# A two-layer attention backbone: the last head of three attention stages put in another order

## The chip, the cores and the metric

The kernel runs on one core of one Trainium2 chip. The time is the device time of one execution in microseconds. A profile of one further execution shows what each engine did; the engines are PE (matrix products), DVE and POOL (elementwise work), ACT (activations and copies) and SP (it issues most DMAs).

## The reference, cut to what matters

512 latent tokens and 256 context tokens of width 1024 go through two layers. In each layer one projection feeds two attentions: A, a two-dimensional neighbourhood attention with 8 heads, and B, a grouped-query attention with 8 query heads and 2 key-value heads. Latent queries also read the context's keys. Both results are multiplied by a SiLU gate, projected, merged and projected again. The context tokens run through layer 0 alone.

```python
def _merge(a_att, b_att, a_z, b_z, g_a, g_b, w_o_a, w_o_b, w_out):
    o_a = (a_att * jax.nn.silu(a_z)) @ w_o_a
    o_b = (b_att * jax.nn.silu(b_z)) @ w_o_b
    merged = jax.nn.sigmoid(g_a) * o_a + jax.nn.sigmoid(g_b) * o_b
    return merged @ w_out

def _layer(x, ctx, ...):
    ...
    a_att = _na_latent(qa, ka, va, cka, cva, rpb, rows)
    ...
    b_att = _gqa_latent(qb, k_all, v_all)
    out_x = _merge(a_att, b_att, a_z, b_z, g_a, g_b, w_o_a, w_o_b, w_out)
    x_new = x + gate_x * out_x
    if update_ctx:
        ...
        ctx = ctx + gate_c * out_c
    return x_new, ctx
```

All is float32. The kernel splits each operand of a product into a high part in a narrower format, and a low part (operand minus high part), and sums three products: high by high, high by low, low by high.

## The kernel before, in words

**Tiles.** A tile of activations has 128 partitions, on which channels or tokens lie. The nine `big` tiles (128 x 3072 floats) hold whole tensors and are handed out again when their last reader is done. Weights come in pieces of 128 x 512: a DMA into `raw` (three buffers), a cast on ACT into the high part `whi`, a subtraction on DVE or POOL into the low part `wlo` (eight buffers each, tags in the pool `wp`). PSUM has eight banks: one for `psf`, two for transposes (`pst`), and five that each stage shares out anew. In the neighbourhood stage that is one `psx`, three for scores (`pss`) and one for values (`psv`); in the grouped stage two score tiles of two banks and one `psv`; in projections five `psx`.

**Layer.** Projections of keys, values and queries come first, then the neighbourhood stage, the projections for the grouped stage, the grouped stage, then the merge: four chunks of the projection of B (`o_chunks("b", ...)`), each of two groups of output channels, and the output projection. Gate projections and the projection of A are `fill`: pieces that stand between the heads so that PE has work.

**A stage's heads.** `pipeline` runs the scores of head h, then the values of head h-1, then some fill. Scores go to a bank; DVE takes the maximum, ACT the exponential, and the normalisation (`softmax_tail`) is on POOL for two of the four query tiles and on DVE for the others. The values of a head need the probabilities transposed: PE writes four transposes into a bank, ACT casts them (`pth`), DVE subtracts (`ptl`): `transpose_split`, 3 to 6 times a head, with two buffers of each tag. Then come the products with the value tensor into `psv`, and `head_out`: ACT copies one half of the bank (`ho`), DVE adds the other half, and the sum is multiplied into the gated tensor (`za` for A, `zb` for B; line 699). The one `psv` bank is free for the next head after the add. In layer 0 each head also has the values of the context queries (`ctx_values`), in the same bank.

**The end of a stage.** After the last head's scores the grouped stage calls `early`: it loads the gate tensors `tg[1]` and `tg[3]`, takes the tiles `gbh` and `gbl` (high and low part of the gated B), and splits the first three quarters of `zb` into them (`hilo`, lines 559 to 569), high parts on ACT, low parts on POOL. Then come the last head's values, and the last quarter. In layer 1's grouped end, and only there, every second split of the last head goes to a score bank and to weight tiles (`spare`), and the product of `head_out` is on DVE. There the chunk weights after the first are also held behind the last head-out's copy on ACT.

**Order.** A planner puts the instructions of each engine in one fixed order, from the program's order and its own costs. `ordered(i, last)` makes it place an instruction behind another one of the same engine. Tiles that don't fit yet wait for the last reader of an older one.

Of the kernel before, what the change touches and what calls it, by code (L numbers as in the profile page):

```python
# [12 lines left out]
ALU = mybir.AluOpType  # L13
# [55 lines left out]
def hybrid_kernel(es: ExitStack, tc, x, ctx, cvec, w_ada, w_ada0, small, gvec, w_in, w_o_a, w_o_b, w_out,  # L69
# [421 lines left out]
    def layer(l, hx, nxt, mid):  # L491
# [67 lines left out]
        def hilo(src, dst, fs, parts=None, lo=lambda f: G, hi_after=None, lo_after=None):  # L559
            sv = src.rearrange("p (f n) -> p f n", f=4)  # L560
            ins = nc.cur_bb.bb.instructions
            for f in fs:
                for a, b in parts or [(0, ntok)]:
                    S.copy(R(dst[0][:, f, a:b]), sv[:, f, a:b])
                    if hi_after is not None and f > 0:
                        ordered(ins[-1], hi_after)
                    lo(f).tensor_tensor(R(dst[1][:, f, a:b]), sv[:, f, a:b], dst[0][:, f, a:b], ALU.subtract)
                    if lo_after is not None and lo(f) is G:
                        ordered(ins[-1], lo_after)
# [4 lines left out]
        def o_chunks(br, prepare, evac):  # L574

            src = (w_o_a if br == "a" else w_o_b)[l]
            act = lambda part, k: gated[br][part][:, k, :]
            res = []
            for i in range(4):
                st = {}  # L580

                def ld(i=i, st=st):
                    st["w"] = load_w2(src, 256 * i, 4, mix_lo)
                pieces = [lambda f=f, n0=n0, n1=n1, i=i, st=st:
                          chan_proj(st["w"], f, act, n0, n1, lambda f, a, b, ps: evac(2 * i + f, a, b, ps))
                          for f in range(2) for n0, n1 in spans]
                res.append((ld, ([prepare] if i == 0 and prepare else []) + pieces))
            return res

# [71 lines left out]
        if True:  # L661
# [11 lines left out]

            def transpose_split(blocks, n0=0, n1=512):

                spare = att["end"] and not first and att["turn"] % 2 == 1
                att["turn"] += 1
                pt = psw(512, "s" if spare else "t")
                for src, c0 in blocks:
                    if c0 is None:  # L680
                        T.transpose(pt.rearrange("p (s n) -> p s n", n=64)[:, 0:8:7, :], src, ident)
                    else:
                        T.transpose(pt[:, c0:c0 + 128], src, ident)  # L683
                pool, th, tl, n = (wp, "whi", "wlo", 8) if spare else (att["p"], "pth", "ptl", att["nt"])
                hi = pool.tile([128, 512], F32R, tag=th, name=nm(th), bufs=n)
                lo = pool.tile([128, 512], F32R, tag=tl, name=nm(tl), bufs=n)
                S.copy(hi[:, n0:n1], pt[:, n0:n1])  # L687
                V.tensor_tensor(lo[:, n0:n1], pt[:, n0:n1], F(hi[:, n0:n1]), ALU.subtract)  # L688
                return hi, lo

            def head_out(po, e, dst):

                n = dst.shape[-1]
                m, o = 64 * e, 64 * (1 - e)
                t1 = att["p"].tile([128, 512], F32, tag="ho", name=nm("ho"), bufs=1)
                S.copy(t1[m:m + 64, :n], po[o:o + 64, :n])
                att["ho"] = nc.cur_bb.bb.instructions[-1].name
                V.tensor_tensor(t1[m:m + 64, :n], po[m:m + 64, :n], t1[m:m + 64, :n], ALU.add)
                (V if (att["end"] and not first) else G).tensor_tensor(dst, dst, t1[m:m + 64, :n], ALU.mult)

            def rows(a, half):
                return a[64 * half:64 * half + 64]
# [53 lines left out]
            def ctx_values(p, vsl, dst, e):  # L756
                hi, lo = transpose_split(
                    [(p[:, 256 * i + 128 * k:256 * i + 128 * k + 128], 256 * k + 128 * i)
                     for k in range(2) for i in range(2)])
                po = psw(256, "v")  # L760
                for k in range(2):
                    T.matmul(po, vsl(4 + k), hi[:, 256 * k:256 * k + 256], start=k == 0, stop=False)
                    T.matmul(po, vsl(4 + k), lo[:, 256 * k:256 * k + 256], start=False, stop=k == 1)  # L763
                head_out(po, e, dst)
# [34 lines left out]
            def na_scores(h, q, kh, kl):  # L799
                load_bias(h)  # L800
                ps_ = []
                for i in range(4):
                    pss = ps_score()
                    qi = q[:, 128 * i:128 * i + 128]
                    at = ((0, 3, 2), (0, 1, 2), (1, 2, 1), (4, 1, -2))[i]
                    for k, b in ((kh, True), (kl, False)):
                        T.matmul(pss.rearrange("p (a b n) -> p a b n", a=2, b=2), qi, blocks_of(k, *at), start=b, stop=not b)  # L807
                    p = p_tile()
                    mx = sp.tile([128, 2], F32, tag="mx", name=nm("mx"), bufs=8)
                    four = lambda a: a.rearrange("p (a b n) -> p a b n", a=2, b=2)  # L810
                    V.tensor_tensor_reduce(four(p[:, :512]), four(pss),
                                           blocks_of(bedg if i == 0 else bint, 0, 1, 1) if i in (0, 2) else four(bint),
                                           -1.0, 3e38, ALU.add, ALU.min, mx[:, 0:1])
                    r = sp.tile([128, 2], F32, tag="r", name=nm("r"), bufs=8)
                    S.activation(p[:, :512], p[:, :512], AF.Exp, bias=mx[:, 0:1], scale=-1.0,
                                 accum_out=r[:, 0:1])
                    softmax_tail(p, 512, r[:, 0:1], [(0, 512)], G if i in NA_POOL else None)
                    ps_.append(p)
                    run(att["bg"], 1)
                return ps_  # L820
# [32 lines left out]
            def pipeline(fill, spread, scores_of, values_of, last=None, bg=[]):  # L853
# [2 lines left out]
                prev = None  # L856
                for h in range(8):
                    att["bg"] = bg if h > 3 or pm["n"] == 1 else []
                    st = scores_of(h)
                    if prev is not None:  # L860
                        values_of(h - 1, prev)
                    run(fill, len(fill) - (n - n * min(h + 1, spread) // spread))
                    prev = st
# [1 line left out]
                    run(fill, len(fill))  # L865
                    last()
                run(bg, len(bg))
                att["end"] = last is not None
                values_of(7, prev)
                run(fill, len(fill))  # L870

            akt = [k_tile(e, True) for e in range(2)]
            att["end"], att["turn"] = False, 0

            def na_first(h):
                j, e = h // 2, h % 2
# [3 lines left out]
                ps_ = na_scores(h, q, kh, kl)  # L880
                return ps_, ctx_scores(q, kh, kl, 256) if first else None

            def values_of(dst, f):
                def g(h, st):
                    vsl = f(h, st[0])
                    if first:
                        e = h % 2
                        zv = dst.rearrange("p (f n) -> p f n", f=4)
                        ctx_values(st[1], vsl, zv[64 * e:64 * e + 64, h // 2, 512:768], e)
                return g  # L890
# [74 lines left out]
            def gq_scores(q, kh, kl):  # L965
                ps_ = []
                for i in range(4):
# [5 lines left out]
                    V.tensor_reduce(mx[:, 0:1], pss, AX, ALU.max, negate=True)  # L973
                    r = sp.tile([128, 2], F32, tag="r", name=nm("r"), bufs=8)
                    S.activation(p, pss, AF.Exp, bias=mx[:, 0:1], accum_out=r[:, 0:1])
                    softmax_tail(p, 768, r[:, 0:1], [(0, 768)], G if i in GQ_POOL else None)
                    ps_.append(p)
                    run(att["bg"], 1)
                return ps_

            def gq_values(h, ps_):
                e, kv = h % 2, h // 4

                def vsl(t):
                    return R(vb[:, t, kv, 64 * e:64 * e + 128])
# [15 lines left out]

            def early():

                for c in (1, 3):
                    tg[c] = big("tg")
                    load_tg(c)
                gated["b"] = hilo_tiles("gb")
                hilo(zb, gated["b"], range(3), lo_after=None if first else att["norm"])
            bg = gate_steps((1,), att["p"]) if first else []
            pipeline(fill, 8, gq_first, values_of(zb, gq_values), early, bg)  # L1010
            gq_es.close()

        with tc.tile_pool(name=f"mrg{l}", bufs=1, reuse_waits="tile") as mp:
# [254 lines left out]
```

## Time and profile before

| | |
|---|---|
| median of 3 runs | 1142.38 us (1141.61 to 1142.96) |
| the profiled execution | 1141.48 us |
| its span, from the first to the last instruction | 1139.6 us |
| busy share of the span | PE 98%, DVE 72%, ACT 51%, POOL 43% |
| granted clock of PE | 0.999 |

A row of a timeline or of the chain of waits begins with its start and its length in microseconds. A name such as `gbl<-zb,gbh` gives the tile written and the tiles read; `xcount` means that neighbours of one kind are merged. A bracket at the end tells how long the engine sat idle before the row, and what ended that. A row of the waits has the waiting engine and tile, what it waited for, the total, the count and the longest.

### The profile page before, as it was taken

The numbers are of one execution on the slowest core, as the hardware profiler recorded it, in microseconds if no ns is written. First come the engines' busy times: TensorE is split into PE (matmuls) and PEld (weight loads), VectorE is DVE, ScalarE is ACT, GpSimd is POOL, SyncE is SP. The second block draws the span as 40 slices with busy tenths as digits, with TensorE's granted clock in tenths as the row PEclk, the third lists the DMA queues.
The fourth block names the chain that finished last, engine by engine and source line by source line (L and its number), as shares of the span: only waits on it lengthen the run. The fifth ranks groups of instructions, "written<-read, shape, count | busy, mean of one in ns | idle before, by whom it ended". The sixth has DMA issues, their size and how long they took to land.

```text
span 1139.6 us, 17434 instructions
## 1 busy us (share of the span) xinstructions
PE 1119.0 (98%) x6128; PEld 947.5 (83%) x6128; DVE 816.4 (72%) x1537; ACT 581.1 (51%) x1185; POOL 492.7 (43%) x467
## 2 busy tenths in 40 slices
PE   7999999999999999999999999999999999999998
PEld 5788888888988888888888887888887988888777
DVE  6777688887554786698588755569787666798783
ACT  6553366665433565666330365337666445665531
POOL 2073354544374343353512427246553664363521
PEclk9999999999999999999999999999999999999999
DMA  9645222333333232461343524634332333141343
GB/s 370 238 127 157 81 61 70 97 115 98 114 102 89 91 108 87 80 242 38 137 141 102 176 75 116 188 91 125 103 111 74 112 94 110 66 157 38 99 163 99
DMA packets 90863, 135.09 MB, mean 119 GB/s; under 512 B 10804, under 2 KB 55064, under 8 KB 90136
## 3 DMA queue, kind: packets, MB, share of 16 engines
q1 hardware_dynamic: 88640, 127.57, 35.2%
q0 software_dynamic: 1856, 6.29, 1.7%
q8 instruction: 48, 0.79, 0.3%
q14 instruction: 39, 0.32, 0.1%
q10 hardware_dynamic: 280, 0.12, 0.0%
HBM read 116.63 MB, written 17.32 MB: 118 GB/s over the span
## 4 chain that ended last, share of the span: by engine, by line
PE 86%; DVE 5%; DMA 3%; issue 3%; POOL 2%; ACT 1%; SPq 0%; POOLq 0%; ACTq 0%; DVEq 0%
PE psx L352 12%; PE psx L354 12%; PE psx L353 12%; PE psf L352 10%; PE psf L354 10%; PE psf L353 10%; PE pst L683 5%; PE pss L807 3%; PE pss L734 2%; PE pss L735 2%; PE psv L990 2%; PE psv L991 2%; PE pst L432 1%; DMA rawb<-in_w_ada_dram 1%; DVE ptl L688 1%
## 5 line engine op out<-in xcount | busy, mean ns | idle before, releaser
L687 ACT CAST pth<-pst 128x512 fp32r<-128x512 f32 (+1 forms) x173 | 97.2, 576 | 96.4 <-PE pst L683 56.0
L688 DVE TENSOR_TENSOR ptl<-pst,pth 128x512 fp32r<-128x512 f32 (+1 forms) x173 | 113.8, 671 | 41.1 <-ACT pth L687 40.0
L339 POOL TENSOR_TENSOR wlo<-raw,whi 128x512 fp32r<-128x512 f32 x68 | 95.9, 1414 | 104.4 <-ACT whi L337 86.2
L352 PE MATMUL psf<-hx,whi 128*128 128x512 f32 (+1 forms) x368 | 140.1, 381 | 0.0
L353 PE MATMUL psf<-hx,whi 128*128 128x512 f32 (+1 forms) x368 | 138.0, 375 | 0.0
L352 PE MATMUL psx<-whi,hx 128*128 128x512 f32 (+1 forms) x368 | 137.8, 375 | 0.0
L354 PE MATMUL psf<-hx,wlo 128*128 128x512 f32 (+1 forms) x368 | 137.7, 374 | 0.0
L354 PE MATMUL psx<-whi,hx 128*128 128x512 f32 (+1 forms) x368 | 135.9, 369 | 0.0
L353 PE MATMUL psx<-wlo,hx 128*128 128x512 f32 (+1 forms) x368 | 135.3, 368 | 0.0
L337 ACT CAST whi<-raw 128x512 fp32r<-128x512 f32 x136 | 82.5, 621 | 55.9 <-DMA raw<-in_w_in_dram 36.5
L322 ACT CAST whi<-raw 128x512 fp32r<-128x512 f32 x88 | 54.0, 622 | 100.9 <-PE psx L354 35.3
L683 PE MATMUL pst<-ident,p 128*128 128x128 f32 x628 | 97.7, 272 | 0.8 <-DVE r L664 0.6
L669 POOL TENSOR_SCALAR r<-r 128x1 f32<-128x1 f32 x64 | 22.3, 348 | 164.1 <-DVE r L664 139.4
L339 DVE TENSOR_TENSOR wlo<-raw,whi 128x512 fp32r<-128x512 f32 x68 | 67.1, 989 | 32.9 <-ACT whi L337 32.6
L325 POOL TENSOR_TENSOR wlo<-raw,whi 128x512 fp32r<-128x512 f32 x36 | 50.7, 1413 | 85.6 <-ACT whi L322 72.4
L683 PEld LDWEIGHTS pst<-ident,p 128*128 128x128 f32 x628 | 76.4, 140 | 12.3 <-PE psv L763 0.7
L670 POOL TENSOR_TENSOR p<-p,r 128x512 f32<-128x512 f32 (+1 forms) x64 | 84.3, 1317 | 5.1
L352 PEld LDWEIGHTS psx<-whi,hx 128*128 128x128 f32 x368 | 69.4, 189 | 12.2 <-issue 1.2
L354 PEld LDWEIGHTS psx<-whi,hx 128*128 128x128 f32 x368 | 69.4, 189 | 12.0 <-DVE hx L1165 0.2
L354 PEld LDWEIGHTS psf<-hx,wlo 128*128 128x128 f32 x368 | 69.3, 188 | 11.8
L353 PEld LDWEIGHTS psx<-wlo,hx 128*128 128x128 f32 x368 | 69.5, 189 | 10.7
L352 PEld LDWEIGHTS psf<-hx,whi 128*128 128x128 f32 x368 | 69.4, 189 | 10.4 <-ACT zt L517 0.2
(265 smaller groups left out, 3068.6 us busy)
## 6 DMA issues: line engine op xcount, KB each, us to landing
raw<-in_w_in_dram SPq DMA_DIRECT2D x168, 256.0 KB, 2.9
rawb<-in_w_ada_dram SPq DMA_DIRECT2D x48, 256.0 KB, 2.9
gs<-zt SPq DMA_DIRECT2D x32, 256.0 KB, 2.0
raw<-in_w_out_dram SPq DMA_DIRECT2D x32, 256.0 KB, 3.0
tg<-gs SPq DMA_DIRECT2D x4, 1536.0 KB, 6.5
rawx<-in_w_ada_dram SPq DMA_DIRECT2D x8, 512.0 KB, 7.7
raw<-in_w_o_a_dram SPq DMA_DIRECT2D x16, 256.0 KB, 2.9
raw<-in_w_o_b_dram SPq DMA_DIRECT2D x16, 256.0 KB, 4.3
```

What stands on the lines that cost most here:

```text
L322: S.copy(hi[:, :n], raw[:, :n])
L325: e.tensor_tensor(lo[:, :n], raw[:, :n], F(hi[:, :n]), ALU.subtract)
L337: S.copy(hi, raw)
L339: lo_eng(i).tensor_tensor(lo, raw, F(hi), ALU.subtract)
L352: T.matmul(ps, lhs[0], rhs[0], start=first, stop=False)
L353: T.matmul(ps, lhs[0], rhs[1], start=False, stop=False)
L354: T.matmul(ps, lhs[1], rhs[0], start=False, stop=last)
L670: G.tensor_tensor(p[:, c0:c1], p[:, c0:c1], r[:, i:i + 1].to_broadcast([128, c1 - c0]), ALU.mult)
L683: T.transpose(pt[:, c0:c0 + 128], src, ident)
L687: S.copy(hi[:, n0:n1], pt[:, n0:n1])
L688: V.tensor_tensor(lo[:, n0:n1], pt[:, n0:n1], F(hi[:, n0:n1]), ALU.subtract)
L807: T.matmul(pss.rearrange("p (a b n) -> p a b n", a=2, b=2), qi, blocks_of(k, *at), start=b, stop=not b)
```

## The change

Layer 0's grouped end: `early` loads only `tg[1]`; `tg[3]` is taken and loaded in the merge, behind the load of the second chunk's weights, in both layers. The high parts of the first three quarters stand behind the last exponential, the low parts behind the last normalisation on POOL. The last head's context values come before its latent values, into a score bank. The product of `head_out` is on DVE at this end of layer 0 too, and the last quarter is split in two pieces (latent and context columns) with the low parts on DVE. The first chunk works its context columns first. The weights of chunks 1 to 3 stand behind the last head-out's copy, in layer 0 as in layer 1.

Layer 1's neighbourhood end: every second split of the last head uses a score bank and weight tiles, and the last query tile's normalisation is on DVE.

```diff
@@ hilo
-                    if hi_after is not None and f > 0:
+                    if hi_after is not None:
                         ordered(ins[-1], hi_after)
@@ o_chunks
-                pieces = [lambda f=f, n0=n0, n1=n1, i=i, st=st:
+                at = [(f, n) for f in range(2) for n in spans]
+                if br == "b" and i == 0:
+                    at.sort(key=lambda x: -x[1][0])
+                pieces = [lambda f=f, n0=n[0], n1=n[1], i=i, st=st:
                           chan_proj(st["w"], f, act, n0, n1, lambda f, a, b, ps: evac(2 * i + f, a, b, ps))
-                          for f in range(2) for n0, n1 in spans]
+                          for f, n in at]
@@ transpose_split
-                spare = att["end"] and not first and att["turn"] % 2 == 1
+                spare = (att["end"] or att["last"]) and not first and att["turn"] % 2 == 1
@@ head_out
-                (V if (att["end"] and not first) else G).tensor_tensor(dst, dst, t1[m:m + 64, :n], ALU.mult)
+                (V if att["end"] else G).tensor_tensor(dst, dst, t1[m:m + 64, :n], ALU.mult)
@@ ctx_values
-                po = psw(256, "v")
+                po = psw(256, "s" if att["end"] else "v")
@@ na_scores
-                    softmax_tail(p, 512, r[:, 0:1], [(0, 512)], G if i in NA_POOL else None)
+                    softmax_tail(p, 512, r[:, 0:1], [(0, 512)],
+                                 G if i in NA_POOL and (first or (h, i) != (7, 3)) else None)
@@ pipeline
                 for h in range(8):
+                    att["last"] = False
...
-                att["end"] = last is not None
+                att["end"], att["last"], att["turn"] = last is not None, True, 0
                 values_of(7, prev)
@@ values_of
-            def values_of(dst, f):
+            def values_of(dst, f, ctx_vsl=None):
                 def g(h, st):
+                    if first and att["end"]:
+                        e = h % 2
+                        zv = dst.rearrange("p (f n) -> p f n", f=4)
+                        ctx_values(st[1], ctx_vsl(h), zv[64 * e:64 * e + 64, h // 2, 512:768], e)
                     vsl = f(h, st[0])
-                    if first:
+                    if first and not att["end"]:
@@ gq_scores
                     S.activation(p, pss, AF.Exp, bias=mx[:, 0:1], accum_out=r[:, 0:1])
+                    att["exp"] = next(x.name for x in nc.cur_bb.bb.instructions[::-1] if x.engine == ON_ACT)
@@ early
-                for c in (1, 3):
-                    tg[c] = big("tg")
-                    load_tg(c)
+                tg[1] = big("tg")
+                load_tg(1)
                 gated["b"] = hilo_tiles("gb")
-                hilo(zb, gated["b"], range(3), lo_after=None if first else att["norm"])
+                hilo(zb, gated["b"], range(3), hi_after=att["exp"], lo_after=att["norm"])
@@ merge
-            hilo(zb, gated["b"], [3], None, lambda f: G if first else V)
+            hilo(zb, gated["b"], [3], spans, lambda f: V)
...
-                        if not first and x.engine == ON_ACT:
+                        if x.engine == ON_ACT:
                             ordered(x, att["ho"])
+                if i == 0:
+                    tg[3] = big("tg")
+                    load_tg(3)
```

More of the change, by code (lines that the diff above doesn't have):

```diff
@@ L872, in layer @@
             akt = [k_tile(e, True) for e in range(2)]
-            att["end"], att["turn"] = False, 0
+            att["end"], att["last"], att["turn"] = False, False, 0
             def na_first(h):
@@ L979, in gq_scores, with gq_vsl @@
                 return ps_
+            def gq_vsl(h):
+                return lambda t: R(vb[:, t, h // 4, 64 * (h % 2):64 * (h % 2) + 128])
             def gq_values(h, ps_):
-                e, kv = h % 2, h // 4
-                def vsl(t):
-                    return R(vb[:, t, kv, 64 * e:64 * e + 128])
+                e = h % 2
+                vsl = gq_vsl(h)
                 po = psw(512, "v")
@@ L1002, in early @@
             def early():
-                for c in (1, 3):
-                    tg[c] = big("tg")
-                    load_tg(c)
+                tg[1] = big("tg")
+                load_tg(1)
                 gated["b"] = hilo_tiles("gb")
-                hilo(zb, gated["b"], range(3), lo_after=None if first else att["norm"])
+                hilo(zb, gated["b"], range(3), hi_after=att["exp"], lo_after=att["norm"])
             bg = gate_steps((1,), att["p"]) if first else []
-            pipeline(fill, 8, gq_first, values_of(zb, gq_values), early, bg)
+            pipeline(fill, 8, gq_first, values_of(zb, gq_values, gq_vsl), early, bg)
             gq_es.close()
```

## The prediction

> **What bounds the kernel now.** I read the page first, then stretches of the span by engine, then PE's waits, the chain of waits and the engines' timelines at the places that the diff touches.
>
> ```profile
> span 1139.6 us, 17434 instructions
> PE 1119.0 (98%) x6128; PEld 947.5 (83%) x6128; DVE 816.4 (72%) x1537; ACT 581.1 (51%) x1185; POOL 492.7 (43%) x467
> ```
>
> PE is the bound: nothing in the diff removes a matmul, so the change can only close or open holes in PE's row. The stretches that it touches are layer 0's grouped end (550 to 562 us), layer 1's neighbourhood end (864 to 883) and layer 1's grouped end (1048 to 1070). The columns below are length, then busy time of each engine with its count.
>
> ```profile
> 550.00:562.00 12.00, 10.03 (x58) 7.93 (x57) 5.92 (x9) 4.78 (x8) 10.13 (x8) 1.00 0.28 94
> 864.00:873.00 9.00, 8.01 (x57) 6.90 (x57) 8.14 (x21) 7.28 (x18) 3.75 (x5) 1.00 0.48 156
> 873.00:883.00 10.00, 8.58 (x52) 6.35 (x51) 6.57 (x10) 5.37 (x10) 3.86 (x4) 1.00 0.01 2
> 1048.00:1062.00 14.00, 13.36 (x82) 10.40 (x81) 10.70 (x20) 10.86 (x23) 9.07 (x9) 1.00 0.00 1
> 1070.00:1090.00 20.00, 20.00 (x90) 16.56 (x89) 16.56 (x20) 9.67 (x17) 8.48 (x6) 1.00 0.41 132
> ```
>
> PE is idle for 1.97, 0.99, 1.42 and 0.64 us in the first four: 5.0 us or 0.44% of the time, so no outcome of this change can be large. PE's waits of the first stretch, and the chain that runs through it:
>
> ```profile
> PE psx L352 <- DVE ho L698: 1.2, 1, 1.2
> PE psf L353 <- POOL gbl L567: 0.8, 1, 0.8
> ```
> ```profile
> 547.25 3.56 issue
> ...
> 550.85 5.88 POOL gbl L567 x3
> ...
> 558.05 1.29 POOL zb L699
> ...
> 560.25 0.50 PE psx L352
> 560.74 0.23 PE psx L353
> ...
> 562.70 0.12 PE psx L353
> ```
>
> The reader is to see a chain on POOL, an engine that is busy 43% of the span: three low parts (gbl, 5.88 us) start only at 550.85, then one weight and one gated product (zb) go in front of the copy that frees the bank PE waits for at 560.25. The last two rows give PE's step: 0.23 us for 512 columns, 0.12 for 256.
>
> **Layer 0's grouped end.** (1) The low parts. They start at 550.85 although their inputs are older; POOL sat idle until the last matmul that reads the first gated tile had gone (the 3.56 us of "issue"), because gbl got that tile's slot among the nine big ones. With tg[3] allocated later, gbh and gbl each move up one freed slot, and the new order puts the low parts behind this normalisation:
>
> ```profile
> 531.19 1.47 POOL L670 TENSOR_TENSOR p<-p,r 128x768 f32<-128x768 f32 x1
> ```
>
> They then run from about 532.7 to 538.6, some 13 us before the first matmul that reads them, and the 0.8 us wait goes. The high parts' new order costs nothing here, since they stand behind the exponentials already.
>
> (2) Context values first, their products in a score bank, the gated product on DVE. The 1.2 us wait was for the context head-out, which was last: it queued behind the latent product on POOL (1.29 us). Now the latent head-out is last, and what is late next is its chain to the last quarter of gbl. Layer 1 has exactly that chain already:
>
> ```profile
> 1070.72 0.58 ACT L696 COPY ho<-psv 64x512 f32<-64x512 f32 x1 [2.01 <-PE psv L991]
> ```
> ```profile
> 1071.33 0.69 DVE L698 TENSOR_TENSOR ho<-psv,ho 64x512 f32<-64x512 f32 x1 [1.90 <-ACT ho L696]
> 1072.06 1.81 DVE L699 TENSOR_TENSOR zb<-zb,ho 64x512 f32<-64x512 f32 x1
> ...
> 1075.49 0.68 DVE L567 TENSOR_TENSOR gbl<-zb,gbh 128x512 fp32r<-128x512 f32 x1
> ```
> ```profile
> 1072.02 3.00 POOL L339 TENSOR_TENSOR wlo<-raw,whi 128x512 fp32r<-128x512 f32 x2 [3.13 <-ACT whi L337]
> ```
>
> From 1070.72 to 1076.17 it takes 5.45 us. PE's cover in layer 0: the context columns of both groups of chunk 0, which need nothing late any more (2 x 12 matmuls x 0.12 = 2.9 us), and three quarters of both 512-column groups (2 x 9 x 0.23 = 4.1 us): 7.0 us. Even with one context group spent before the chain starts, 5.5 us are left. In layer 1 PE did not stop beside the chain (20.00 of 20.00 us in the last stretch above). So I take both waits as gone.
>
> The product of 1.81 us ran beside the two POOL weights of the last row, where it would else take about the 0.69 of the add before it. The Trainium skill speaks against this edit: its page "SBUF — State Buffer", section "Who interferes with whom", says that a DVE instruction with two SBUF inputs and a GpSimd instruction that reads SBUF block each other for a whole instruction. Layer 0's chunk weights, now also behind the head-out, put POOL low parts right there. By that rule the low part that closes the chain could wait once more, for the 1.3 us of a POOL weight: an estimate of 6.8 us for the chain, still under 7.0, and 1.3 us of loss if one context group is spent early. The 1.81 us agrees with the rule; my sum keeps the 5.45.
>
> (3) The last quarter in two pieces on DVE, which is 5.92 of 12.00 busy: inside the chain above. (4) Chunk weights 1 to 3 behind the head-out: ACT and DVE have room (4.78 and 5.92 of 12), and chunk 1 isn't read before chunk 0's 8.4 us (24 x 0.23 + 24 x 0.12) are through: nothing. On SP the raws of chunks 2 and 3 and those of the output projection queue behind these casts; they are read 8 to 16 us later: nothing; were one late, a landing of 2.9 us (the last row quoted below) is the upper end. (5) tg[3], 1.5 MB, leaves a stretch that is full of transfers for one with a DMA share of 0.28, and is first read by chunk 2: nothing, in both layers.
>
> Bounds for this end: a gain of 1.97 (all of PE's idle) down to 0.8 (the low parts alone); I take 2.0, rounded, since layer 1's row is the nearest.
>
> **Layer 1's neighbourhood end.** The last head's four splits alternate between the two transposing banks and spare score banks, and the spare ones take a weight tile's place. Head 7 now needs, in the chain of waits:
>
> ```profile
> 879.68 0.50 PE psv L837
> ...
> 881.36 0.54 ACT pth L687
> ...
> 883.07 0.14 PE psx L352
> ```
>
> That is 3.39 us where its 12 matmuls need about 1.7 (4 x 0.23 and 8 x about 0.1). With the splits made ahead the gain is 0 to 1.7; I take 1.3. The last normalisation moves from POOL to DVE: on DVE at most the 0.69 of the add above, before transposes that wait for other things; between 0 and +0.7 I take +0.1, since DVE is 6.57 of 10.00 busy there.
>
> The spare tiles cost something that the diff doesn't show. Weight tiles are taken in program order. In layer 1's grouped end, which has spares already, chunk 0's weights are issued at 1002.52 but cast only behind the third spare:
>
> ```profile
> 1002.52 0.57 SPq L334 DMA_DIRECT2D raw<-in_w_o_b_dram  x1
> ```
> ```profile
> 1060.28 0.59 ACT L687 CAST whi<-pss 128x512 fp32r<-128x512 f32 x1
> 1060.76 1.14 ACT L337 CAST whi<-raw 128x512 fp32r<-128x512 f32 x2
> ```
>
> So the key-value weights of the next projection, and the query weights behind them, will now be cast after head 7's second spare and no longer before it. Two things follow. A whole group of that projection fills PE between 867 and 872 now (8 of each of three kinds, and 24 x 0.12 = 2.9 us); it won't be at hand:
>
> ```profile
> L352 PE MATMUL psf<-whi,hx 128*128 128x256 f32 x8 | 2.3, 292 | 0.0
> ```
>
> What PE then idles can be refilled up to the 1.42 us of the stretch 873 to 883; cost 0 to 2.9, I take 1.4. Against it, these weights' low parts leave DVE, which is 8.14 of 9.00 us busy there:
>
> ```profile
> 861.63 1.28 DVE L325 TENSOR_TENSOR wlo<-raw,whi 128x512 fp32r<-128x512 f32 x2
> ...
> 866.83 0.96 DVE L325 TENSOR_TENSOR wlo<-raw,whi 128x512 fp32r<-128x512 f32 x1
> ```
>
> 2.24 us: a gain of 0 to 2.24, I take 1.0, as only part lies on the last scores' way. Net: -1.3 + 0.1 + 1.4 - 1.0 = -0.8.
>
> **Layer 1's grouped end.** The first two high parts of gbh have to stand behind the last exponential, where PE lives from split to split:
>
> ```profile
> 1048.97 1.14 ACT L564 CAST gbh<-zb 128x512 fp32r<-128x512 f32 x2
> ```
>
> Cost 0 to 1.14 us; ACT is idle for 3.1 of the 14 us, so I take +0.3. Everything else of this end (product and last quarter on DVE, spares, order of the weights) is as it was.
>
> **Sum.** -2.0 - 0.8 + 0.3 = -2.5 us. The profiled execution took 1141.48, 0.90 below the median of the runs, 1142.38; the median becomes 1139.9. Around the span of 1139.6 lie 1.9 us that nothing here touches. All bounds together reach from -5.9 (1.97, 1.7 and 2.24 gained) to +7 (0.8 gained; 2.9, 0.7, 2.9 and 1.14 lost), D's late weights aside.
>
> **Rivals.** (B) More: all of the neighbourhood end's gain comes, the key-value work finding its place later (-1.7 - 2.24 with no filler lost, somewhat less in practice): 1137.5. For it: DVE carries that stretch. (C) No change: the wait is replaced. The context columns are worked off before the latent head-out, and PE then waits for the bank that its add frees (0.58 + 0.69 = 1.3 us instead of 1.2): only the 0.8 of the low parts stays, and the neighbourhood end gives nothing: 1141.8. For it: matmuls of chunk 0 fill PE between the values now too. (D) Slower: the key-value weights come late. If the second spare is copied where the fourth split is now (881.36), the filler is lost (2.9), the first weight needs its cast (0.6, half of the pair at 1060.76) and a POOL low part (1.3, as the product at 558.05), so that the first matmul stands at 883.8, 0.7 late, and the fourth of four weights, for which there is no raw buffer before 883.8, still has to be loaded, some 2.3 us more behind a group's first 18 matmuls (2.2 us): landing, cast and a DVE low part (0.68 above) end 4.3 us after the buffer comes free, by this row of the page's transfers:
>
> ```profile
> raw<-in_w_in_dram SPq DMA_DIRECT2D x168, 256.0 KB, 2.9
> ```
>
> Together 5.9 us: 1142.4 - 2.0 + 0.3 + 5.9 = 1146.6, less if groups are interleaved, 1145 as its middle. It ends slower from 4.0 us in that stretch on. Against it: spare banks are free long before 881, so the plan can copy early.
>
> **Numbers.** The forecast's own case, 1138.6 to 1141.3, has 0.50; B 0.19, C 0.17, D 0.14. A measurement of this kernel can tell about 0.2%, 2.3 us, from no change: faster means under 1140.1. That takes B and 0.31 of the forecast's case: faster 0.50, same 0.19 + 0.17 = 0.36, slower 0.14. The range 1137.0 to 1143.9 leaves out D and a small part of B.
>
> **What would show it.** Layer 0: gbl on POOL right behind the last normalisation, no PE wait on gbl or ho near 550 to 562, PE idle there near 0. Neighbourhood end: splits in whi tiles, L837 to L847 of head 7 without holes, key-value casts (L337) after them, no key-value matmuls between 867 and 872. Grouped end of layer 1: PE idle about 0.3 us above the 0.64 of before. I am wrong if the key-value projection starts with PE waiting for whi or wlo, or if new holes stand far from these three ends, since a plan that is made anew can move other instructions.

## The result, and the profile after

The change made the kernel slower: 1148.03 us in the median of 4 runs (1146.54 to 1149.99), against 1142.34 before (4 runs too); the ratio is 1.0051, with a 95% interval of 1.0033 to 1.0069. That is 5.7 us more where 2.5 us less was forecast, outside the range and on its other side. The profiled execution of after took 1148.96 us and has a span of 1147.0.

The page of after:

```profile
span 1147.0 us, 17415 instructions
PE 1121.6 (98%) x6128; PEld 950.2 (83%) x6128; DVE 819.5 (71%) x1542; ACT 582.2 (51%) x1186; POOL 487.4 (42%) x462
```

The matmuls are the same 6128; what grew is the holes in PE's row and the length of some matmuls. A number used below is "PE's stalls": for each matmul the time to the next one's start, less the usual step of its shape (the lower quartile of all steps of that shape), summed over a stretch. Matmuls that step more slowly at a lower clock count too. Over the whole span they went from 43.0 to 50.3 us, nearly the 7.4 us between the two spans. By stretch, before to after: layer 0's grouped end (530 to 575 us) 3.4 to 3.1, layer 1's neighbourhood end (850 to 900) 5.9 to 11.1, layer 1's grouped end (1040 to 1090) 3.7 to 5.1; the merge of layer 1 and some scattered places make up the rest. The loss is in one stretch, and the gain at layer 0's end is missing. The windows of after (length, then busy time and count of PE, PEld, DVE, ACT and POOL, then the granted clock, DMA share, GB/s):

```profile
550.00:562.00 12.00, 10.69 (x70) 9.29 (x70) 9.13 (x12) 5.67 (x11) 3.70 (x4) 1.00 0.67 236
864.00:873.00 9.00, 7.58 (x48) 5.86 (x48) 7.71 (x22) 6.67 (x16) 3.02 (x5) 1.00 0.08 29
873.00:883.00 10.00, 7.03 (x48) 5.71 (x47) 5.76 (x9) 5.93 (x12) 5.43 (x4) 0.99 0.28 85
883.00:890.00 7.00, 5.95 (x25) 5.57 (x26) 3.61 (x6) 3.23 (x7) 1.74 (x2) 0.52 0.51 148
```

Between 873 and 883 PE idles 3.0 us where it idled 1.4, and then comes something that before does not have anywhere near: from 883 to 890 the granted clock is 0.52, and 25 matmuls fill the time in which 60 ran before. Of the 5.2 us more in this end, 2.7 lie between 884 and 890, where no matmul waits and each one's step is longer.

**What happened at the neighbourhood end.** PE's waits in it (860 to 892 us), and ACT's and SP's timelines:

```profile
PE psv L841 <- DVE ho L701: 1.5, 1, 1.5
PE psf L352 <- ACT whi L337: 1.1, 1, 1.1
PE psf L353 <- POOL wlo L339: 1.0, 1, 1.0
PE psv L846 <- DVE ptl L691: 0.9, 1, 0.9
PE pss L686 <- POOL p L673: 0.6, 1, 0.6
```
```profile
872.77 1.03 ACT L690 CAST whi<-pss 128x512 fp32r<-128x512 f32 x2 [0.36 <-PE pss L686]
873.68 1.67 ACT L337 CAST whi<-raw 128x512 fp32r<-128x512 f32 x3
875.24 0.98 ACT L690 CAST pth<-pst 128x448 fp32r<-128x448 f32 x2
880.26 0.62 ACT L337 CAST whi<-raw 128x512 fp32r<-128x512 f32 x1 [4.04 <-DMA raw<-in_w_in_dram]
...
881.39 0.58 ACT L690 CAST pth<-pst 128x512 fp32r<-128x512 f32 x1
...
882.52 0.58 ACT L699 COPY ho<-psv 64x512 f32<-64x512 f32 x1
```
```profile
876.29 0.39 SPq L334 DMA_DIRECT2D raw<-in_w_in_dram  x1
```

Read it from the top. The spare copies take two weight tiles at 872.77; the key-value weights (L337) follow them at 873.68, three of them, since there are three raw buffers. Only when one of these is free can the fourth load be issued, at 876.29. Before, its row stood 33 us earlier, and its cast was done at 847:

```profile
843.27 0.37 SPq L334 DMA_DIRECT2D raw<-in_w_in_dram  x1
```
```profile
846.65 0.63 ACT L337 CAST whi<-raw 128x512 fp32r<-128x512 f32 x1
```

The fourth cast waits for its load, and ACT executes in order: ACT stands still for 4.04 us while head 7's splits (881.39) and head 6's sum (882.52) are queued behind it. PE has nothing left, for the groups that it would fill with need the same weight.

**Layer 0's end.** Both old waits are gone, and the low parts moved to where the forecast put them (532.64 us, POOL). Two new waits took their place, the first at 536 us, the second at 557:

```profile
PE psf L352 <- ACT whi L337: 1.3, 1, 1.3
PE psv L1002 <- DVE ptl L691: 0.8, 1, 0.8
```
```profile
532.64 3.71 POOL L567 TENSOR_TENSOR gbl<-zb,gbh 128x768 fp32r<-128x768 f32 x2
```
```profile
533.98 2.52 DVE L670 TENSOR_SCALAR p<-p,r 128x256 f32<-128x256 f32 x2
536.41 0.68 DVE L691 TENSOR_TENSOR ptl<-pst,pth 128x512 fp32r<-128x512 f32 x1
```
```profile
557.00 0.58 ACT L699 COPY ho<-psv 64x512 f32<-64x512 f32 x1 [1.77 <-PE psv L1002]
557.60 1.14 ACT L337 CAST whi<-raw 128x512 fp32r<-128x512 f32 x2
```

The pair of context normalisations on DVE takes 2.52 us beside the low parts on POOL; the same pair in before:

```profile
534.08 0.61 DVE L667 TENSOR_SCALAR p<-p,r 128x256 f32<-128x256 f32 x2
```

The split behind it is late by that much. At 557 the next group in PE's order is one of chunk 1, in the `psf` bank. Of chunk 0 only one context group has run by then (12 matmuls, 554.36 to 555.75, which used both of its weights); its other three groups follow from 558.85 on, in the `psx` banks. Chunk 1's weights now stand behind the head-out's copy, and PE waits for the first of them, cast at 557.60.

**Layer 1's grouped end.** The high parts went behind the last exponential, as read beforehand, and there they stand in front of a split for which PE waits:

```profile
1059.26 0.90 ACT L984 ACTIVATE p<-pss,mx 128x768 f32<-128x768 f32 x1
...
1060.15 1.13 ACT L564 CAST gbh<-zb 128x512 fp32r<-128x512 f32 x2
1061.18 1.07 ACT L690 CAST pth<-pst 128x512 fp32r<-128x512 f32 x2
```
```profile
PE psv L1001 <- ACT pth L690: 0.7, 1, 0.7
```

### The profile page after: what moved, and what is told of

Same layout as the page of the kernel before. It is cut to its first block, busy times and chain, and to the rows that moved or that the text cites. A ratio compares the mean times of both kernels' runs of the same rounds, so it can differ in the third digit from the quotient of the medians.

```text
span 1147.0 us, 17415 instructions
## 1 busy us (share of the span) xinstructions
PE 1121.6 (98%) x6128; PEld 950.2 (83%) x6128; DVE 819.5 (71%) x1542; ACT 582.2 (51%) x1186; POOL 487.4 (42%) x462
## 4 chain that ended last, share of the span: by engine, by line
PE 86%; DVE 4%; issue 3%; DMA 3%; ACT 2%; POOL 1%; SPq 0%; POOLq 0%; ACTq 0%
PE psx L352 12%; PE psx L354 12%; PE psx L353 12%; PE psf L352 10%; PE psf L353 10%; PE psf L354 10%; PE pst L686 5%; PE pss L810 2%; PE pss L737 2%; PE pss L738 2%; PE psv L1002 2%; PE psv L1001 2%; PE pst L432 1%; DMA rawb<-in_w_ada_dram 1%; DMA raw<-in_w_in_dram 1%
## 5 line engine op out<-in xcount | busy, mean ns | idle before, releaser
L337 ACT CAST whi<-raw 128x512 fp32r<-128x512 f32 x136 | 82.5, 621 | 60.2 <-DMA raw<-in_w_in_dram 39.1
L322 ACT CAST whi<-raw 128x512 fp32r<-128x512 f32 x88 | 54.0, 622 | 99.9 <-PE psx L354 36.3
L686 PEld LDWEIGHTS pst<-ident,p 128*128 128x128 f32 x622 | 75.6, 141 | 12.5 <-PE psv L766 0.7
L673 POOL TENSOR_TENSOR p<-p,r 128x768 f32<-128x768 f32 (+1 forms) x63 | 83.0, 1317 | 5.0
```

The costliest lines, as they stand in the source:

```text
L322: S.copy(hi[:, :n], raw[:, :n])
L337: S.copy(hi, raw)
L673: G.tensor_tensor(p[:, c0:c1], p[:, c0:c1], r[:, i:i + 1].to_broadcast([128, c1 - c0]), ALU.mult)
```

## The experiments

Medians are of 5 to 11 runs; the ratio is to runs of the kernel before on the same chip (medians 1142.14 to 1142.43). "Base" is e4.

| run | what it is | us | ratio, 95% interval | stalls 530-575 | 850-900 | 1040-1090 |
|---|---|---|---|---|---|---|
| e1 | after, no spare places | 1143.46 | 1.0008, 0.9999 to 1.0017 | 3.0 | 5.8 | 5.1 |
| e2 | before, spare places only | 1147.25 | 1.0040, 1.0026 to 1.0054 | 3.4 | 10.1 | 3.8 |
| e3 | after, spare banks without weight tiles | 1143.23 | 1.0009, 1.0000 to 1.0018 | 3.1 | 5.8 | 5.0 |
| e4 | e1, layer 1's high parts free | 1141.75 | 0.9993, 0.9985 to 1.0002 | 3.1 | 5.9 | 3.7 |
| e5 | after, fourth cast behind a split (no effect) | 1149.02 | 1.0058, 1.0045 to 1.0071 | 3.1 | 10.9 | 5.1 |
| e9 | the same, behind the right split | 1146.11 | 1.0033, 1.0021 to 1.0045 | 3.1 | 8.1 | 5.1 |
| e12 | after, key-value weights first | 1144.37 | 1.0016, 1.0007 to 1.0025 | 3.1 | 7.8 | 5.1 |
| e6 | base, layer 0's chunk weights free | 1140.79 | 0.9988, 0.9980 to 0.9997 | 1.5 | 5.9 | 3.7 |
| e7 | base, context values last | 1145.21 | 1.0027, 1.0017 to 1.0037 | 5.1 | 6.0 | 3.8 |
| e8 | base, layer 0's low parts on DVE | 1141.37 | 0.9995, 0.9986 to 1.0003 | 2.5 | 6.0 | 3.7 |
| e10 | e6 and e8 together | 1141.28 | 0.9991, 0.9982 to 0.9999 | 2.1 | 5.9 | 3.8 |
| e11 | e10, the normalisation back on POOL | 1141.31 | 0.9991, 0.9982 to 0.9999 | 2.1 | 5.9 | 3.7 |
| e13 | e6 with spare places, key-value weights first | 1141.78 | 0.9999, 0.9990 to 1.0008 | 1.5 | 7.5 | 3.8 |

Theory: the spare places of the neighbourhood end carry the loss, because they hold weight tiles. Rival: it is spread over the grouped ends, or comes from the normalisation on DVE.

**e1 and e2: the spare places out, and alone.**

```diff
-                spare = (att["end"] or att["last"]) and not first and att["turn"] % 2 == 1
+                spare = att["end"] and not first and att["turn"] % 2 == 1
```

> The changed kernel with one part undone: layer 1's neighbourhood end takes no spare places (every split uses its own score bank and split tiles again); everything else, the normalisation on VectorE too, stays. Theory (the spare places hold weight tiles, so the key-value weights come late and ScalarE stands 4.04 us on the fourth of them in front of the last heads' work, after which the granted clock falls): TensorE's stalls from 860 to 890 us go from 10.9 back to about 5, so 5 to 6 us shorter than the changed kernel, 1142 to 1143, and no ScalarE idle time on a weight DMA in that stretch. Rival 1 (the loss is spread over layer 0's and layer 1's grouped ends): under 2 us shorter, 1146 or more. Rival 2 (the normalisation on VectorE delays the last splits): the stretch stays above 8 us of stalls.

e2 is the kernel before with `att["last"]`, the count of turns and the normalisation of the diff added.

> The kernel before with that one part added: spare score bank and spare weight tiles for every other split of layer 1's last neighbourhood head, the count of splits started at 0 there, and the last normalisation of that head on VectorE; nothing of the two grouped ends. Theory: this alone carries the loss, 1147 to 1148, with the stalls of TensorE and the ScalarE idle time of 4 us behind the fourth key-value weight as in the changed kernel. Rival 1: within 1.5 us of the kernel before (1141 to 1144), the loss coming from elsewhere or only together with the other parts.

Taking them out gives back 4.6 us, and adding them to the kernel before costs 4.8. The part is necessary and sufficient for most of the loss, and the spread-out rival falls. e1 keeps the normalisation on DVE and has 5.8 us of stalls there, so the second rival falls too.

**e3: the second bank without the weight tiles.**

```diff
-                pool, th, tl, n = (wp, "whi", "wlo", 8) if spare else (att["p"], "pth", "ptl", att["nt"])
+                pool, th, tl, n = (wp, "whi", "wlo", 8) if spare and att["end"] else (att["p"], "pth", "ptl", att["nt"])
```

> The changed kernel, but the splits that use the spare score bank in layer 1's neighbourhood end write their halves to the split tiles of their own (two of each) and not to weight tiles; the grouped ends keep both. Theory (the weight tiles are the harm, the bank is not): as without spare places or a little better, 1141.5 to 1143, the key-value casts again ahead of the last two heads' splits. Rival (the second bank lets the transposes run ahead of work that PE needs first, or takes the bank that the filler uses): stays above 1145.

It is at e1, 0.2 us apart: with split tiles of their own the banks do no harm and bring nothing. The harm is in the weight tiles. PE's waits in that stretch say why the banks bring nothing, first of the kernel before, then of e3:

```profile
PE pst L681 <- DVE ptl L688: 1.1, 2, 0.8
PE psv L837 <- DVE ho L698: 0.9, 1, 0.9
```

```profile
PE psv L841 <- DVE ho L701: 2.4, 2, 1.5
PE psv L846 <- DVE ptl L691: 0.2, 1, 0.2
```

The 1.1 us on splits are gone, and 1.5 us more on the bank of the sums stand in their place: the splits were not the last thing to be late, the one bank `v` of the value products was.

**e4: layer 1's high parts free.** `hi_after=att["exp"] if first else None`, on top of e1.

> The changed kernel without spare places in the neighbourhood end and with the high parts of layer 1's grouped end free again (only layer 0's are ordered behind the last exp). Theory: ScalarE's two casts of 0.57 us each go back to the gap that the trace of before had them in (1056.8), and the splits of the last head start 1.1 us earlier: 0.8 to 1.4 us shorter than the kernel without spare places alone, 1141 to 1142. Rival (they are hidden as my sum took it): within 0.4 us of it.

1.71 us shorter than e1: a little more than expected. The two casts do not go back to the gap but far ahead of this end, where ACT has room, and its stalls fall by 1.4:

```profile
1025.06 0.61 ACT L564 CAST gbh<-zb 128x512 fp32r<-128x512 f32 x1
1032.88 0.61 ACT L564 CAST gbh<-zb 128x512 fp32r<-128x512 f32 x1
```

**e5 and e9: the block in ACT's order.** The key-value weight's cast is needed late; the kernel's plan put it early.

```diff
+            at = len(nc.cur_bb.bb.instructions)
             w = load_w2(W, C_BKV, KT, mix_lo)
             w_q = load_w(W, C_BQ, 512, 4, bq_lo) + ...
+            if not first:
+                for x in [x for x in nc.cur_bb.bb.instructions[at:] if x.engine == ON_ACT][3:]:
+                    ordered(x, att["split"])
```

> The changed kernel with its spare places kept, but the fourth key-value cast and the query casts ordered on ScalarE behind the last split of the last neighbourhood head. It tells apart what a late weight costs by itself from what its cast costs as a block in ScalarE's order. Theory A (the block is the loss: 4.04 us of ScalarE standing still ahead of head 6's copy and head 7's splits): that idle time goes, the last head runs on while the weight lands, and 3 to 5 us come back: 1143 to 1145. Theory B (my prediction's rival as it was worked out: TensorE itself lacks the key-value weights, whatever ScalarE does): the stall only moves to the key-value groups, under 1.5 us come back: 1146 or more.

This was a miss of the edit, not of the theory: the last split of the program is one of the two that go to weight tiles, and ACT had made it at 874 us. The order of the rest stayed, and e5 is a second measurement of the changed kernel. In e9 `att["split"]` is the last split with a tile of its own.

> The changed kernel with its spare places, the fourth key-value cast and the query casts ordered on ScalarE behind the last split that goes to a split tile of its own (882.25 to 883.98 us in the run before this one, whose order was behind a split into a weight tile that was done at 874 and so moved nothing). Theory A (the block in ScalarE's order is the loss): the idle time of about 4 us ahead of head 6's copy goes; 3 to 5 us come back, 1143 to 1145. Theory B (TensorE lacks the key-value weights whatever ScalarE does): the stall moves to the key-value groups behind the last head, under 1.5 us come back, 1146.5 or more.

1.9 us below after, 2.9 below e5: between the two theories, nearer the second. ACT no longer stands on the load:

```profile
878.77 0.59 ACT L690 CAST pth<-pst 128x512 fp32r<-128x512 f32 x1 [2.39 <-PE pst L686]
879.63 0.58 ACT L701 COPY ho<-psv 64x512 f32<-64x512 f32 x1 [0.27 <-PE psv L854]
...
880.67 0.62 ACT L337 CAST whi<-raw 128x512 fp32r<-128x512 f32 x1
```

The holes at POOL's low part (1.0) and at the fourth weight's low part (1.0, in place of 0.3) stay. How much of the 1.9 us is the block's own price stays open, because the clock changed too. All six runs of e9 had a mean granted clock of 0.999 or more; of the four runs of after only one did, and it took 1146.54, 0.4 above e9's median. The stalls say the same: without the 2.7 us of slow matmuls after has 8.5 from 850 to 900, and e9 has 8.1. So, as far as one run and two profiles show it, most of what e9 gains is a clock that no longer falls; at the same clock the late weights cost nearly as much without ACT's standstill.

**e12: the key-value weights ahead of the spare tiles.** `load_w2(W, C_BKV, KT, mix_lo)` is called just before the last head's values, so that the spare tiles are given out behind it. Nothing else moves in the program.

> The changed kernel, all parts kept, but layer 1's key-value weights are loaded and split ahead of the last neighbourhood head in the program, so that the two spare weight tiles come behind them in the order in which weight tiles are given out. Theory (the place of the spare tiles in that order is the whole of the loss: it delays the casts, the raw tiles, the fourth load, and then ScalarE's order): the fourth key-value cast comes before 870 us, no idle time of ScalarE on a weight load in the stretch, TensorE's stalls from 850 to 900 us back to 6 or less, 1142 to 1143.5, as without spare places. Rival (what the cast's order left over, some 3 us, is the spare places' own: splits running ahead of the value chain and taking VectorE and PE out of turn): 1145 or more, with no weight late.

3.7 us come back of the 4.6 that leaving the spare places out gives, a time between the two expected. The fourth weight is cast early again:

```profile
847.65 0.62 ACT L337 CAST whi<-raw 128x512 fp32r<-128x512 f32 x1
```

So the place in the order of the weight tiles is most of the cause. 0.9 us is left. The profiled execution is the slowest of e12's eleven (1146.46): the granted clock fell once more (0.50 from 880 to 886), and its 7.8 us of stalls hold about 2 of slow matmuls. The seven runs at 0.999 or more have a median of 1143.68, 0.2 above e1. e13 asks the same without the other losses:

> The best of the single runs (layer 1's high parts free, layer 0's chunk weights free: 1140.8) with the spare places back and the key-value weights ahead of them. If the spare places are worth anything once the weights are not behind them, under 1140.4; if the second place gains nothing (with split tiles of its own it gained 0.2), 1140.4 to 1141.2; if the query weights, now behind the spare tiles, come late in their turn, 1141.5 or more.

e13 is 1.0 us above e6, 0.9 among the runs at 0.999 or more, and its profiled execution had a clock of 1.0. So with the key-value weights in front the spare places still lose 0.2 to 1.0 us. The time lies where the expectation put late query weights, and the trace shows them. Their first casts (L322), made from 856 to 866 us in e6, now come right behind the spare splits, in front of head 6's last splits:

```profile
872.58 1.02 ACT L690 CAST whi<-pss 128x512 fp32r<-128x512 f32 x2
873.49 1.15 ACT L322 CAST whi<-raw 128x512 fp32r<-128x512 f32 x2
874.53 0.98 ACT L690 CAST pth<-pst 128x448 fp32r<-128x448 f32 x2
```

On DVE the low part of one of them (1.55 us at 874.67) stands in front of the same splits, and PE waits 1.2 us for their low parts. It is the same displacement once more, one projection later. This is read from the trace; no run put the query weights in front as well.

**e6: layer 0's chunk weights free.** `if not first and x.engine == ON_ACT:`, as in the kernel before.

> The kernel without spare places and with layer 1's high parts free, and besides with the casts of the second and later chunk weights of layer 0's grouped projection free of the order behind the head-out copy. Theory: the 1.3 us wait of a group on a weight cast behind the copy (556.6 us) goes, and since the value chain's multiply stays on VectorE the old wait of 1.2 us on the last head's sum comes back at most in part: 0.3 to 1.3 us shorter than the kernel it is built on (1141.75), 1140.5 to 1141.4. Rival (the casts stand ahead of the head-out copy again, and what the order cost it had saved): within 0.4 us of it, with a wait on the head-out's sum in place of the one on the cast.

0.96 us shorter: nine matmuls of chunk 1's group run from 556.77 to 558.62, where PE waited. The wait on the head-out's sum does not come back: its one wait near here is the 0.7 us at 536. Layer 0's end has 1.5 us of stalls, 1.9 less than before.

**e7: context values last again.**

> The same base (no spare places, layer 1's high parts free), with the context values of layer 0's last grouped head behind its main values again, as in the kernel before; the output columns still context first. Theory: the 0.8 us wait on a split at 536 us goes, because the two context normalisations that take 2.52 us beside POOL's low parts are no longer needed first, but the context chain ends last again, so a wait on its sum at the start of the projection comes back: from 0.5 us shorter to 1.0 us longer than 1141.75. Rival (the context first carries the whole gain of layer 0's part): 1.5 us or more longer.

3.5 us longer than its base, of which 2.0 are stalls of this stretch. The profiled execution has the other 1.5 in the first 50 us of the span, far from the edit, where those of all kernels here scatter between 11.0 and 12.5; so what the order costs beyond 2.0 is not shown. PE's waits:

```profile
PE psx L352 <- DVE ho L701: 1.7, 1, 1.7
PE psv L1002 <- DVE ptl L691: 0.8, 1, 0.8
```

The wait on the context head-out's sum is back, as expected, but its price was taken too low. The 0.8 us wait stays, against the expectation: it is on a value split that DVE has queued behind the two slowed normalisations, in either order. Context first carries layer 0's gain.

**e8: the low parts on DVE.** `lo=lambda f: V if first else G` in `early`.

> The same base, with the low parts of layer 0's first three gated columns on VectorE and not on POOL, so that nothing of POOL's runs beside the two context normalisations. Theory (the normalisations are slowed by POOL's three low parts beside them, 2.52 us for the two where they took 0.61): they take under 0.8 us, the 0.8 us wait at 536 us goes, unless VectorE's three low parts (about 1 us each) stand ahead of a split there: 0.3 to 0.9 us shorter than 1141.75. Rival (the duration is not POOL's doing): the two still take over 2 us together.

With POOL out of the way the two normalisations take 0.66 us and the wait at 536 is gone; 0.38 us of the median is within its uncertainty, the stalls fall by 0.6.

```profile
535.34 0.66 DVE L670 TENSOR_SCALAR p<-p,r 128x256 f32<-128x256 f32 x2
```

**e10 and e11: the parts together.**

> What the single runs favour, together: the changed kernel without spare places in layer 1's neighbourhood end, layer 1's high parts free, layer 0's chunk weights free of the head-out copy, and layer 0's first three low parts on VectorE. The base of the single runs was 1141.75; freeing the weights gave 0.96 and the low parts on VectorE 0.38: 1140.4 if they add, about 1.8 under the kernel before. Rival (VectorE becomes the bound once it has the low parts and the weights' low parts beside them): 1140.8 or more.

> The one before, with the last normalisation of layer 1's neighbourhood back on POOL. My prediction had it cost 0.1 us to have it on VectorE, and the spare places needed it: within 0.5 us of the one before. Rival (it delays VectorE's splits in that stretch): over 0.5 us shorter.

They don't add: e10 is 0.5 us above e6, within the intervals, and 0.6 above it in the stalls. DVE now makes the low parts while POOL normalises. In both runs that normalisation takes 2.04 us in place of 1.47; in e8 it starts behind most of DVE's two low parts (1.82 us), in e10 soon after they begin, and they take 3.09. PE waits 1.3 us for the split behind them.

```profile
531.25 3.09 DVE L567 TENSOR_TENSOR gbl<-zb,gbh 128x768 fp32r<-128x768 f32 x2
534.27 0.68 DVE L691 TENSOR_TENSOR ptl<-pst,pth 128x512 fp32r<-128x512 f32 x1
```

Where the normalisation of layer 1 runs makes 0.03 us. The best version is e6: 0.9988 of the kernel before, 1.4 us, with an interval that leaves out 1.

## Why the prediction was wrong, step by step

- **Layer 0's end, -2.0; measured -0.3 in the stalls.** Steps (1) and (2) held: both waits went, context first is worth 2.0 us in the stalls (e7), and the chain of the last quarter was covered. Step (4) failed: "chunk 1 isn't read before chunk 0's 8.4 us are through: nothing". It took it that all of chunk 0 comes first, but PE's order has a group of chunk 1 behind only 12 of chunk 0's 48 matmuls (1.4 of the 8.4 us); PE reached it at about 556.8, before the copy at 557.00, and waited 1.3 us. With the weights free (e6) the stalls are 1.9 lower than before, which is the -2.0; the median is 1.4 lower. Step (1) missed that moving POOL's low parts puts them beside two DVE normalisations that PE needs: 0.8.
- **Neighbourhood end, -0.8; measured +5.2 in the stalls, +4.6 to +4.8 by e1 and e2.** The term of the spares, -1.3, was zero (e3), since the bank of the value products was late next; the normalisation, +0.1, was zero (e11); the weights' low parts did leave DVE (7.71 us busy from 864 to 873 in place of 8.14), but no run shows that this gained the 1.0. What failed is the term "cost 0 to 2.9, I take 1.4" for the lost filler. It saw that the weights would come behind the spare tiles, but priced only one group that ran between 867 and 872. It did not follow the three raw buffers on to the fourth load, nor ask what ACT holds back when the fourth cast waits. In its place the weights' delay cost 3.7 us (e12), together with the clock that fell in three of four runs, for which the sum had no term. Rival D followed the buffers, and its 5.9 us is near the 5.2; but it made this depend on the second spare being copied at 881.36. The copy was made at 872.77, early, as the argument against D said, and the fourth load was late all the same. So D needed no such condition, and a chance of 0.14 was too low. That the two sums are so near is partly luck: 2.7 of the 5.2 are matmuls at half clock, which D didn't have.
- **Layer 1's grouped end, +0.3; measured +1.4 in the stalls, 1.7 by e4.** The mechanism was right and the size at or above the upper bound of 1.14: a busy share of ACT over 14 us says nothing about the one place between two splits.
- **The sum.** -0.3, +5.2 and +1.4 give +6.3 of the 7.3 us by which the stalls of the two profiled executions differ; the medians differ by 5.7, as the profiled execution of after was 0.9 above its median and that of before 0.9 below.

The profile of before could have shown it: the rows at 843.27 and 846.65 say that the fourth key-value weight was ready some 17 us before the stretch in question, so that "behind the second spare" meant a delay of 25 us and more and not one of a few.

## What to carry to other kernels

When a tile is borrowed from a pool that is given out in program order, list everything that comes later from that pool and from the pools that feed it, and find in the profile of before when each of them happened; the cost is their delay, not the borrowed tile's. An instruction that waits for a load holds back whatever its in-order engine has behind it, so look up that queue as well, but what that costs is seen only against runs at the same clock. A split or copy that is made earlier brings nothing while the next thing in PE's order, here a single bank, is free no sooner.

## What the runs showed of the hardware

**The clock fell without a long hole.** In after, PE was busy for 0.72 and 0.51 us of two neighbouring stretches of 2 us, and the granted clock went to half. By what the five clock figures below lack of 1.00, it was there for about 6.8 us. The longest single wait of PE there was 1.5 us:

```profile
880.00:882.00 2.00, 0.72 (x4) 0.53 (x4) 0.69 (x1) 1.74 (x4) 0.43 (x1) 1.00 0.12 45
882.00:884.00 2.00, 0.51 (x5) 0.31 (x3) 1.99 (x4) 1.61 (x3) 0.85 (x1) 0.72 0.47 136
884.00:886.00 2.00, 1.95 (x5) 1.56 (x6) 0.53 (x1) 0.27 (x1) 1.28 (x1) 0.50 0.81 252
886.00:888.00 2.00, 2.00 (x11) 2.00 (x10) 0.69 (x1) 0.96 (x2) 0.00 (x0) 0.50 0.01 5
888.00:890.00 2.00, 2.00 (x13) 2.00 (x12) 1.39 (x2) 1.36 (x4) 0.47 (x1) 0.58 0.63 149
```

e2 has nearly the same holes, and in its profiled execution the clock stayed at full speed:

```profile
882.00:884.00 2.00, 0.45 (x4) 0.25 (x4) 2.00 (x4) 1.44 (x3) 0.78 (x2) 1.00 0.56 140
```

Of e2's five runs, three had a mean clock of 1.0 (1146.31, 1146.31 and 1147.25 us) and two of 0.997 (1147.86 and 1148.06): the fall comes in some executions, and these two are 1.3 us longer in the mean. After and e5, whose order is the same there, give nine runs: one at 1.0 (1146.54), two at 0.998 (1147.10, 1147.67), six at 0.996 or 0.997 (1148.85 to 1149.99). So of the 5.7 us of the result some 1.5 go with the clock; that estimate rests on the one run at full speed. All six runs of e9, whose holes are shorter, had 0.999 or more. The Trainium skill, "TensorE: Matmul & The Clock Gate", "What's actually happening", says that the clock halves after an idle window of about 3.4 us, and that this window is free-running, so that one kernel differs from run to run. The runs agree with the second in that they differ; on the first the traces show that PE need not be idle throughout, since matmuls ran in each of these stretches.

**DVE beside POOL.** The pair of normalisations took 0.61 us alone, 2.52 beside POOL's low parts, and 0.66 once these were on DVE (e8); the pair of low parts on DVE took 1.82 us in e8 and 3.09 in e10. The rule of the Trainium skill, "SBUF — State Buffer", "Who interferes with whom", which the prediction weighed only at the gated product, names both kinds of instruction, and these rows agree with it.
